# Transformer block in split float32: down operands formed as sums, six up tiles in seven products, one more product ahead of the last phase

## Chip, cores, metric

One core of a Trainium2 chip runs the program. The metric is device time in microseconds (us) of one execution, the median of several. The engines are TensorE (PE, with its weight loads PEld), VectorE (DVE), ScalarE (ACT), GpSimd (POOL) and SyncE (SP, which only issues DMAs here).

## What is computed

One layer of an encoder trunk, 512 tokens by 1024 columns, all in float32: three groups of attention heads, one output projection, a gated MLP with a depthwise convolution, and a gated embedding. The change lies in the MLP:

```python
def conv_gated_mlp(h, w_up, conv_w, conv_b, w_down):   # h 512x1024, w_up 1024x5632, w_down 2816x1024
    u = h @ w_up
    up = jnp.pad(u, ((0, 0), (CONV_WIDTH - 1, 0), (0, 0)))
    c = conv_b
    for j in range(CONV_WIDTH):                         # CONV_WIDTH = 3
        c = c + conv_w[j] * up[:, j:j + S]
    gate, val = jnp.split(c, 2, axis=-1)
    return (jax.nn.silu(gate) * val) @ w_down
...
    h = h + conv_gated_mlp(rms_norm(h, ln_ffn[i]), w_up[i], conv_w[i], conv_b[i], w_down[i])
    gate = jax.nn.sigmoid(rms_norm(h, ln_ple[i]) @ w_ple_gate[i])
    h = h + (p[i] @ w_ple_proj[i]) * gate
```

## The kernel before

**Split operands.** Every float32 operand of a product is split in two parts: `hi`, a rounded copy that ACT writes, and `lo`, the rest, which DVE writes (`split`, line 168). A product is three matmuls, hi·hi, hi·lo and lo·hi (`mm3`). So each weight tile goes through a chain: a load into a raw tile by SP, the copy on ACT, the subtraction on DVE, then PE. There are 6 raw tiles of 768 columns (`NRAW`, line 151) and 7 pairs of hi and lo. They are used in turn, so a load waits until the tile six places back has been split, and a split until the pair seven places back has been multiplied.

**Up projection.** It goes in 22 tiles `f` of 128 gate and 128 value columns. In a plain tile (`up_plain`, line 1237) each half is 8 blocks times 3 matmuls of 512 token columns: 48 matmuls from 2048 columns of weights, in three pieces. In a tile in seven products (`up_seven`, line 1261) the 2x2 block product of Strassen and Winograd stands in place of eight block products: 7 products of 12 matmuls with 256 columns, 84 in all. Its weights (`seven_weights`, line 1102) are 3584 columns in five raw tiles. Three adding transfers from HBM, issued by POOL, and four POOL additions of 256 columns form the sums among them. The products are accumulated in PSUM banks X, Y, Z and Z2; ACT copies them out and DVE adds them into SBUF tiles `su`. `SEVEN` (line 50) names the tiles done so: 5, 10 and 15. They are woven with plain tiles, a piece of a plain tile after the second (third product in program text), and so on.

**Convolution and left operands.** `ff_chain` starts each half on ACT and adds two taps on DVE (`c<-u`, or `c<-su` for a tile in seven products), then multiplies the halves. PSUM banks are few: two of kind z, two s, three t, one o. A plain tile's gate half stands in a z bank until its two taps have read it. Two tiles `f` and `f + 1` make one pair; `left` (line 1194) forms from it the seven left operands of the down projection, four of them sums `sm`, and splits them.

**Down projection.** The 22 tiles fall into four phases (`PHASES`, line 46: tiles 0 to 5, 6 to 11, 12 to 17, 18 to 21). For each phase and half `n` of the output columns there are seven products (`PRODUCTS`, line 937), each 18 matmuls of 256 columns (12 in phase 3), into banks X, Y, Z. Behind each product DVE adds the bank into the residual `h` (`add_h`); the next product in the same bank waits for that. Phase 0 and phase 1 are done in a block of 14 products each, in the middle of the up tiles; phases 2 and 3 together at the end, which I call the last phase. The right operands come from `down_weights` (line 1120): four blocks are loaded, and four differences t1 to t4 are made by POOL in place, each from tiles that earlier splits and differences have read. In phases 0 to 2 they lie in raw tiles of 768 columns; in phase 3 in tiles of 512 named `dn_a`, `dn_b`, `dn_t`.

**Order.** Every step is a `Task` with a cost, dependencies and slots. PE's order is the order in which the program makes the PE tasks. For the other engines a small planner (`trial`, line 1645, and the loop behind it) sets a fixed order from costs and due times. Each engine then runs its queue in order; POOL's queue holds sums and adding transfers alike, and a transfer's issue waits there for what it needs. The loop from line 1500 sets the order of up tiles: a tile of `SEVEN` starts when plain tiles are `AHEAD` (2) behind, and a down block when its tiles have been done for three tiles (`downs`). In front of phase 3 stand four products of phase 2: a1, t1, a2 of half 0 and a1 of half 1. Then `cols3` transposes `h` on PE (`n_t<-ident,h`) for the final gate, once the additions into its rows are made, and `gate` (`pg`, line 1565) follows.

Of the kernel before, what the change touches and what calls it, by code (L numbers as in the profile page):

```python
# [47 lines left out]
AHEAD = 2  # L48

SEVEN = (5, 10, 15)  # L50
# [3 lines left out]
def kernel(ctx: ExitStack, tc: tile.TileContext, x, xt0, xt, pt_in, small, g_ffn_in, bias_c,  # L54
# [875 lines left out]
    L1A, L2A, L2B, L3, L1, L2, L4 = range(7)  # L930
    G, LEFT = {}, {}

    def left_tiles(name):
# [3 lines left out]
    PRODUCTS = ((L1A, 0, "X", True), (L1, 4, "Y", True), (L2, 5, "X", False), (L4, 2, "Y", False),  # L937
                (L3, 6, "X", False), (L2A, 1, "Z", True), (L2B, 3, "X", False))
# [8 lines left out]

    ADDS = {0: ((0, 0),), 1: ((1, 1),), 2: ((0, 1),), 3: ((0, 1),), 4: ((1, 1),), 5: ((0, 0),), 6: ((1, 0),)}

    def add_h(n, j, acc):  # L950
        for b, c in ADDS[j]:
            dve.tensor_tensor(out=hblk(b, n, c), in0=hblk(b, n, c), in1=pv(acc), op=ALU.add)
# [90 lines left out]

    def split_of(w, deps=(), gain=None, group=None, i=0):

        w.hi_slot = Slot("hi") if group is None else group.slot
        makes = [w.hi_slot] if not w.hi_slot.users else []

        def do():
            w.hi, w.lo = split(w.t, w.n, gain, None if group is None else group.get(i, w.n))  # L1050

        w.split = Task("do", [AC(w.n), DV(w.n * (1 if gain is None else 1.12))], do, (w.load, *deps), makes, [w.raw] + ([] if makes else [w.hi_slot]))
        return w

    def again(r, name, deps):
# [8 lines left out]
        w.hi_slot = Slot("hi")  # L1064
        w.split = Task("do", [AC(w.n), DV(w.n)], do, (w.load, *deps), [w.hi_slot], [w.raw])
# [52 lines left out]
    RIGHT = {"a1": 0, "t1": 4, "t2": 5, "b2": 2, "t3": 6, "a2": 1, "t4": 3}  # L1118

    def down_weights(ph, n, name, tag="raw"):  # L1120

        m = w_down[ph].shape[4]
        src = {what: w_down[ph][n, i, j] for what, (i, j) in (("a1", (0, 0)), ("b1", (0, 1)), ("b2", (1, 1)), ("a2", (1, 0)))}
        raw = {what: tile_of(m, f"{name}_{what}", src.get(what), tag) for what in ("a1", "b1", "b2", "t2", "a2")}

        place = {what: what for what in raw}
        wrote, read = {what: [q.load] for what, q in raw.items()}, {what: [] for what in raw}

        def diff(what, to, a, b):

            a, b, place[what] = place[a], place[b], to

            def do():
                x, y, z = (raw[q].t[:, :m] for q in (to, a, b))
                pool.tensor_tensor(out=x, in0=y, in1=z, op=ALU.subtract)

            q = Task("do", [("pool", 0.3 + m * 0.0021)], do, wrote[a] + wrote[b] + wrote[to] + read[to], (),
                     list({raw[p].raw: 0 for p in (to, a, b)}))
            for p in (a, b):
                read[p].append(q)  # L1140
            wrote[to], read[to] = [q], []

        def take(what):
            if what in ("t1", "t2", "t3", "t4"):
                diff(what, *{"t1": ("a1", "b1", "a1"), "t2": ("t2", "b2", "t1"), "t3": ("b1", "b2", "b1"), "t4": ("a2", "a2", "t2")}[what])
            p = place[what]
            w = again(raw[p], f"{name}_{what}", wrote[p])
            read[p].append(w.split)
            return w

        return take
# [42 lines left out]
    def left(f):  # L1194
# [6 lines left out]
        def one():  # L1201
# [7 lines left out]
            tt(out=sm[:, 0], in0=r1[:, :H], in1=r1[:, H:], op=ALU.subtract)  # L1209
            tt(out=sm[:, 1], in0=r1[:, H:], in1=r2[:, H:], op=ALU.add)  # L1210
            act.copy(hi[:, L1A], r1[:, :H])
            act.copy(hi[:, L2A : L2B + 1], r2.rearrange("p (j c) -> p j c", j=2))

        def two():
            (r1, r2), (hi, lo), sm = v["r"], v["hl"], v["sm"]
            tt(out=sm[:, 2], in0=sm[:, 1], in1=r1[:, :H], op=ALU.subtract)
            tt(out=sm[:, 3], in0=r2[:, :H], in1=sm[:, 2], op=ALU.subtract)
            act.copy(hi[:, L3:], sm)

        def three():  # L1220
            (r1, r2), (hi, lo), sm = v["r"], v["hl"], v["sm"]
            tt(out=lo[:, L1A], in0=r1[:, :H], in1=f32(hi[:, L1A]), op=ALU.subtract)
            tt(out=lo[:, L2A : L2B + 1], in0=r2.rearrange("p (j c) -> p j c", j=2), in1=f32(hi[:, L2A : L2B + 1]), op=ALU.subtract)

        def four():
            (r1, r2), (hi, lo), sm = v["r"], v["hl"], v["sm"]
            tt(out=lo[:, L3:], in0=sm, in1=f32(hi[:, L3:]), op=ALU.subtract)
# [96 lines left out]
    class Down:  # L1324
# [6 lines left out]
        def product(self, what, phs=None, last=True):  # L1331

            j = tuple(RIGHT).index(what)
            li, ri, an, begins = PRODUCTS[j]
            assert ri == RIGHT[what]
# [23 lines left out]
            if last:  # L1359
                self.reads[an] = [Task("do", [DV(S)], lambda: add_h(self.n, j, self.accs[an]), [p], (), [self.slots[an]])]  # L1360
                H_ADDS[self.n, j] = self.reads[an][0]

    def down(ph, n, tags):
        d = Down((ph,), n, tags)
        for what in RIGHT:
# [104 lines left out]
    PLAIN = [f for f in range(2, NF) if f not in SEVEN]  # L1470
    plain = (f for f in PLAIN for _ in up_plain(f))
    at_f, pieces = [2], [0]
    DT = {"X": "t", "Y": "o", "Z": "t"}
    due = {}

    def count():

        for ph in due:
            due[ph] += 1
        for ph in range(2):  # L1480
            if ph not in due and all(f in done_f for f in range(PHASES[ph], PHASES[ph + 1])):
                due[ph] = 0

    def fill(n):
# [254 lines left out]
```

## Time and profile before

| | us |
|---|---|
| median of 3 runs (727.46 to 729.07) | 727.47 |
| the profiled execution | 727.97 |
| its span in the trace | 726.2 |
| PE, DVE, ACT, POOL busy | 706.1, 553.0, 393.8, 270.9 |
| up tiles begin | 314 |
| first down block | 430.7 to 460.7 |
| second down block | 515.4 to 545.8 |
| last phase | 620.0 to 676.0 |
| gate | 676.0 to the end |

How to read the rows that follow: `out<-in` names tiles with their numbers left out. All lines carry one line number, L78, that of the helper which issues every instruction, so they are told apart by their tiles: `u` and `pg` are plain up tiles and the gate, `sX`, `sY`, `sZ` the products of a tile in seven, `dn_X`, `dn_Y`, `dn_Z` the down products, `w_raw`, `w_hi`, `w_lo` weights on their way, `g_ah`, `g_al` (or `xh`, `xl` in the last phase) left operands. A matmul's duration in a row includes its way through the array. What a matmul takes of PE's time is read from start to start. DVE's instructions overlap by a little in the same way, so the sum of mean durations is a little above the busy time.

### The profile page before, as it was taken

Reading aid. Unit: us, or ns where it says so; the run is one execution under the profiler, and the core shown is the slowest. Engines: PE = TensorE matmul, PEld = TensorE weight load, DVE = VectorE, ACT = ScalarE, POOL = GpSimd, SP = SyncE. Lnnn points to the kernel's source line nnn. Section 1 sums busy time; section 2 is a strip of 40 time slices with the busy share of each in tenths; the row PEclk is TensorE's granted clock in tenths of the full one; section 3 lists DMA queues with packets and bytes.
Section 4 is the critical chain, followed back from the end, with each engine's and each line's share of the span. In section 5 each row is a group of like instructions: output and inputs, shape, how many; then the busy total and the mean of one; then the engine's idle time right before and its main releaser. Section 6 shows DMA issues by size and latency. Waiting matters only on the chain. (4 is left out here: it accounts for less than half of the span.)

```text
span 726.2 us, 11876 instructions
## 1 busy us (share of the span) xinstructions
PE 706.1 (97%) x4219; PEld 633.7 (87%) x4219; DVE 553.0 (76%) x1085; ACT 393.8 (54%) x745; POOL 270.9 (37%) x359
## 2 busy tenths in 40 slices
PE   9998999999999999999999999999999999999997
PEld 8987989998999887889888899888998888899886
DVE  7678787887877855758978768787898779988552
ACT  6646775865766664564655544543444543544821
POOL 5676676756665640212101144031520004361400
PEclk9999999999999999999999999999999999999999
DMA  9443425404211135564445434562254322123441
GB/s 332 172 136 110 120 63 124 138 30 110 88 48 56 59 63 165 171 210 90 138 138 125 102 100 123 139 159 66 88 175 117 95 87 82 57 73 94 156 129 58
DMA packets 36806, 83.22 MB, mean 115 GB/s; under 512 B 4198, under 2 KB 5990, under 8 KB 36748
## 3 DMA queue, kind: packets, MB, share of 16 engines
q1 hardware_dynamic: 32700, 73.52, 32.3%
q0 software_dynamic: 3760, 8.66, 6.4%
q8 instruction: 33, 0.54, 0.3%
q10 hardware_dynamic: 288, 0.30, 0.1%
q14 instruction: 25, 0.20, 0.1%
HBM read 74.19 MB, written 4.21 MB: 108 GB/s over the span
## 5 line engine op out<-in xcount | busy, mean ns | idle before, releaser
L78 DVE TENSOR_TENSOR w_lo<-w_raw,w_hi 128x768 fp32r<-128x768 f32 (+1 forms) x118 | 114.9, 993 | 21.9 <-ACT w_hi L78 21.2
L78 ACT CAST w_hi<-w_raw 128x768 fp32r<-128x768 f32 (+1 forms) x118 | 89.6, 786 | 71.1 <-POOL w_raw L78 33.0
L78 PE MATMUL u<-Tl,w_hi 128*128 128x512 f32 (+1 forms) x336 | 125.6, 374 | 0.8 <-DVE Tl L78 0.8
L78 PE MATMUL u<-Th,w_hi 128*128 128x512 f32 (+1 forms) x336 | 125.7, 374 | 0.6 <-ACT pps L78 0.6
L78 PE MATMUL u<-Th,w_lo 128*128 128x512 f32 (+1 forms) x336 | 125.4, 373 | 0.0
L78 POOL TENSOR_TENSOR w_raw<-w_raw,w_raw 128x768 f32<-128x768 f32 (+1 forms) x30 | 55.0, 1854 | 143.7 <-DVE w_lo L78 112.8
L78 PEld LDWEIGHTS u<-Tl,w_hi 128*128 128x128 f32 x336 | 63.1, 188 | 13.0 <-DVE Tl L78 1.2
L78 PEld LDWEIGHTS u<-Th,w_hi 128*128 128x128 f32 x336 | 63.1, 188 | 12.9 <-ACT pps L78 1.0
L78 PEld LDWEIGHTS u<-Th,w_lo 128*128 128x128 f32 x336 | 63.1, 188 | 12.5
L78 DVE SCALAR_TENSOR_TENSOR c<-u,cols,c 128x511 f32<-128x511 f32 x76 | 56.7, 747 | 18.6 <-ACT c L78 17.4
L78 POOL DMA_DIRECT2D w_raw<-in_w_up_dram x9 | 7.9, 912 | 100.2 <-DMA w_raw<-in_w_up_dram 100.2
L78 ACT ACTIVATE c<-u,cols 128x512 f32<-128x512 f32 x38 | 29.5, 776 | 21.7 <-PE u L78 21.7
L78 PE MATMUL dn_X<-w_hi,g_ah 128*128 128x256 f32 x144 | 40.7, 283 | 0.3 <-DVE h L78 0.3
L78 PE MATMUL dn_X<-w_lo,g_ah 128*128 128x256 f32 x144 | 40.7, 283 | 0.3 <-DVE w_lo L78 0.3
L78 PE MATMUL dn_X<-w_hi,g_al 128*128 128x256 f32 x144 | 40.6, 282 | 0.0
L78 PE MATMUL B_z<-B_h,Th 128*128 128x384 f32 x96 | 34.6, 360 | 0.6 <-DVE B_zn L78 0.6
L78 PE MATMUL C_z<-C_h,Th 128*128 128x384 f32 x96 | 34.3, 358 | 0.0
L78 PE MATMUL C_z<-C_l,Th 128*128 128x384 f32 x96 | 32.3, 337 | 0.0
L78 PE MATMUL B_z<-B_h,Tl 128*128 128x384 f32 x96 | 32.3, 337 | 0.0
L78 PE MATMUL C_z<-C_h,Tl 128*128 128x384 f32 x96 | 32.3, 337 | 0.0
L78 PE MATMUL B_z<-B_l,Th 128*128 128x384 f32 x96 | 32.3, 337 | 0.0
L78 PEld LDWEIGHTS dn_X<-w_hi,g_ah 128*128 128x128 f32 x144 | 27.1, 188 | 0.8 <-ACT w_hi L78 0.5
(484 smaller groups left out, 2145.6 us busy)
## 6 DMA issues: line engine op xcount, KB each, us to landing
w_raw<-in_w_up_dram SPq DMA_DIRECT2D x50, 384.0 KB, 3.7
w_raw<-in_w_down_dram SPq DMA_DIRECT2D x24, 384.0 KB, 3.1
w_raw<-in_w_up_dram SPq DMA_DIRECT2D x22, 256.0 KB, 3.4
B_r<-in_w_in_dram SPq DMA_DIRECT2D x12, 384.0 KB, 3.4
C_r<-in_w_in_dram SPq DMA_DIRECT2D x12, 384.0 KB, 3.2
wo_r<-in_w_out_dram SPq DMA_DIRECT2D x16, 256.0 KB, 2.9
w_raw<-in_w_ple_gate_dram SPq DMA_DIRECT2D x16, 256.0 KB, 2.9
h<-in_x_dram SPq DMA_DIRECT2D x4, 512.0 KB, 7.0
```

The lines of the kernel that those rows point to most:

```text
L78: ins = getattr(self.eng, op)(*a, **k)
```

## The change

- Tiles 4, 7, 9, 11, 13 and 15 are done in seven products instead of 5, 10 and 15.
- The order of pieces is one written string: P is a piece of a plain tile (three a tile), S one of a tile in seven (six), D one product of a down block. Between the two down blocks stand three plain tiles and three in seven, in alternation. The last 17 pieces are plain.
- The seven products of the down projection are formed another way. The right operands are named by sums of blocks: 1e, 1o, 2o as loaded, S1, 1e2e, S2 and 1oS2 as sums. In the 768-column phases S1 and 1e2e are made by an adding transfer from HBM onto a loaded block, S2 and 1oS2 by POOL; in phase 3 all four by POOL. Five blocks are loaded where four were. The signs go to the left operands and to `add_h`, which now also subtracts.
- In front of phase 3 stand five products of phase 2: 1e, S1, 1o of half 0, and 1e, S1 of half 1. The transposes `cols3` are placed elsewhere among the last products; those of the second half now stand between the last down product and the gate.

`LO_BY` is empty, so `lo_by_dma`, which is new too, is never used.

```diff
-AHEAD = 2
-
-SEVEN = (5, 10, 15)
+ORDER = ("PPPPSSPSSSPSPPPPSSPSSSPSPSSPSSSPSPDDDDDDDDDDDDDDSSPSSSPSPSSPSSSPSPSSPSSSPSPDDDDDDDDDDDDDDPPPPPPPPPPPPPPPPP")
...
+BY = {"S1": "dma", "1e2e": "dma", "S2": "pool", "1oS2": "pool"}
...
-    PRODUCTS = ((L1A, 0, "X", True), (L1, 4, "Y", True), (L2, 5, "X", False), (L4, 2, "Y", False),
-                (L3, 6, "X", False), (L2A, 1, "Z", True), (L2B, 3, "X", False))
+    PRODUCTS = {"1e": (0, "X", True, 1, 0, ALU.add), "S1": (3, "Y", True, 0, 1, ALU.subtract), "S2": (4, "X", False, 0, 0, ALU.add),
+                "1o": (2, "Z", True, 1, 0, ALU.add), "1e2e": (5, "X", False, 0, 1, ALU.subtract), "1oS2": (1, "Y", False, 0, 0, ALU.add),
+                "2o": (6, "X", False, 1, 1, ALU.subtract)}
...
     def down_weights(ph, n, name, tag="raw"):
...
-        def diff(what, to, a, b):
...
-                pool.tensor_tensor(out=x, in0=y, in1=z, op=ALU.subtract)
...
+        by = {what: BY[what] if tag == "raw" else "pool" for what in BY}
+        firsts = {"S1": "2e", "1e": "1e", "1o": "1o", "1e2e": "1e" if by["1e2e"] == "dma" else "2e", "2o": "2o"}
...
+        def add(what, to, other, before=()):
+            if by[what] == "dma":
+                v = (lambda: src[other]) if what in ("S1", "1e2e") else (lambda: raw[other].t[:, :m])
+                more = () if what in ("S1", "1e2e") else [raw[other].raw]
+                deps[what] = [add_of(raw[to], 0, m, v, before, more)]
+            else:
+                deps[what] = [sum_of(raw[to], 0, raw[other], 0, m, before)]
...
+            if what == "S2":
...
+                add("S2", "1e", "S1", [*deps["S1"], *deps.get("1e2e", ()), w["1e"].split])
+            if what == "1oS2":
+                add("1oS2", "1o", "1e", [*deps["S2"], w["1o"].split])
...
     def left(f):
...
-            tt(out=sm[:, 0], in0=r1[:, :H], in1=r1[:, H:], op=ALU.subtract)
-            tt(out=sm[:, 1], in0=r1[:, H:], in1=r2[:, H:], op=ALU.add)
+            tt(out=sm[:, 0], in0=r1[:, H:], in1=r1[:, :H], op=ALU.subtract)
+            tt(out=sm[:, 2], in0=r2[:, :H], in1=r1[:, :H], op=ALU.subtract)
...
-            tt(out=sm[:, 2], in0=sm[:, 1], in1=r1[:, :H], op=ALU.subtract)
-            tt(out=sm[:, 3], in0=r2[:, :H], in1=sm[:, 2], op=ALU.subtract)
+            dve.scalar_tensor_tensor(sm[:, 1], sm[:, 0], -1.0, r2[:, :H], ALU.mult, ALU.subtract)
+            dve.scalar_tensor_tensor(sm[:, 3], sm[:, 1], -1.0, r2[:, H:], ALU.mult, ALU.subtract)
...
+    FIRST = ("1e", "S1", "1o"), ("1e", "S1")
...
-    for what in ("a1", "t1", "a2"):
-        d0.product(what, (2,), False)
-    d1.product("a1", (2,), False)
-    for what in RIGHT:
-        d0.product(what, (3,) if what in ("a1", "t1", "a2") else None)
+    d0, d1 = DL
+    for what in PRODUCTS:
+        d0.product(what, (3,) if what in FIRST[0] else None)
+    d1.product("1e", (3,))
     cols3(0, 0)
     cols3(1, 0)
-    d1.product("a1", (3,))
+    d1.product("S1", (3,) if "S1" in FIRST[1] else None)
     cols3(2, 0)
-    d1.product("a2")
     cols3(3, 0)
-    for what in ("t1", "t2", "b2", "t3"):
+    for what in ("S2", "1o", "1e2e", "1oS2"):
         d1.product(what)
+    d1.product("2o")
     cols3(0, 1)
     cols3(1, 1)
-    d1.product("t4")
```

More of the change, by code (lines that the diff above doesn't have):

```diff
@@ L46, with tiles_of @@
 PHASES = (0, 6, 12, 18, 22)
-AHEAD = 2
-SEVEN = (5, 10, 15)
+ORDER = ("PPPPSSPSSSPSPPPPSSPSSSPSPSSPSSSPSPDDDDDDDDDDDDDDSSPSSSPSPSSPSSSPSPSSPSSSPSPDDDDDDDDDDDDDDPPPPPPPPPPPPPPPPP")
+def tiles_of(order):
+    f, n, tiles = 2, {"P": 0, "S": 0}, {"P": [], "S": []}
+    for c in order:
+        if c in n:
+            if n[c] == 0:
+                tiles[c].append(f)
+                f += 1
+            n[c] = (n[c] + 1) % {"P": 3, "S": 6}[c]
+    assert f == NF and not any(n.values()), (f, n)
+    return tiles["P"], tiles["S"]
+PLAIN, SEVEN = tiles_of(ORDER)
+LO_BY = ()
+BY = {"S1": "dma", "1e2e": "dma", "S2": "pool", "1oS2": "pool"}
 @with_exitstack
@@ L1331, in product @@
         def product(self, what, phs=None, last=True):
[L1333 to L1335 removed]
+            li, an, begins = PRODUCTS[what][:3]
             for ph in phs or self.phs:
```

136 lines of the change are left out of this document (64 added, 72 removed).

## Prediction

> **What bounds the kernel now.** I read the page's head first, then busy time by stage, then the waits, and last the instructions in order of time around each wait.
>
> ```profile
> span 726.2 us, 11876 instructions
> PE 706.1 (97%) x4219; PEld 633.7 (87%) x4219; DVE 553.0 (76%) x1085; ACT 393.8 (54%) x745; POOL 270.9 (37%) x359
> ```
>
> TensorE (PE) is busy for 97% of the span; the others have room on the average. The change touches only what follows the first up tiles: the changed program issues the same PE instructions in the same order until the middle of the up projection. These are that part's stretches (columns: length, busy time and instructions of PE, PEld, DVE, ACT, POOL, clock, DMA share, GB/s). The bounds are where the PE stream changes kind: up tiles 2 to 9, first down block, up tiles to the second block, that block, the remaining up tiles, the last phase.
>
> ```profile
> 339.60:430.70 91.10, 91.10 (x475) 77.19 (x474) 73.55 (x108) 47.75 (x73) 18.36 (x17) 1.00 0.46 123
> 430.70:460.70 30.00, 30.00 (x254) 29.95 (x253) 24.50 (x32) 12.41 (x17) 9.51 (x5) 1.00 0.51 156
> 460.70:515.40 54.70, 54.70 (x278) 45.91 (x278) 43.71 (x63) 27.75 (x42) 12.23 (x10) 1.00 0.37 96
> 515.40:545.80 30.40, 30.07 (x253) 29.90 (x252) 26.86 (x34) 12.57 (x17) 9.88 (x5) 1.00 0.52 155
> 545.80:620.00 74.20, 74.20 (x320) 59.68 (x319) 61.67 (x84) 33.45 (x50) 10.17 (x5) 1.00 0.33 96
> 620.00:681.00 61.00, 58.70 (x472) 56.78 (x470) 50.38 (x64) 31.48 (x50) 22.05 (x17) 1.00 0.26 83
> ```
>
> Up to 620 us PE has no gap worth the name, at full granted clock (1.00): there only fewer or shorter products help. The last phase is the one place where PE waits. VectorE (DVE) is next: 81% in the first stretch, 80% in the third.
>
> **The change, part by part.**
>
> *Three more up tiles in seven products.* A plain tile is 48 matmuls of 512 columns, a seven-product tile 84 of 256. The first row is 216 matmuls in one piece of the chain of work that ended last (start, us, what); the others are the first matmuls of neighbouring pieces around one seven-product tile (start, duration).
>
> ```profile
> 545.99 50.41 PE u L78 x216
> ```
>
> ```profile
> 409.58 0.28 PE L78 MATMUL sX<-Th,w_hi 128*128 128x256 f32 x1
> 413.83 0.39 PE L78 MATMUL u<-Th,w_hi 128*128 128x512 f32 x1
> 418.02 0.28 PE L78 MATMUL sY<-xh,w_hi 128*128 128x256 f32 x1
> 422.29 0.40 PE L78 MATMUL u<-Th,w_hi 128*128 128x512 f32 x1
> 425.09 0.28 PE L78 MATMUL sX<-xh,w_hi 128*128 128x256 f32 x1
> 426.51 0.44 PE L78 MATMUL u<-Th,w_hi 128*128 128x512 f32 x1
> ```
>
> 50.41 / 216 = 0.2334 us each, so 11.20 us for a plain tile. The seven-product tile takes (413.83 - 409.58) + (422.29 - 418.02) + (426.51 - 425.09) = 4.25 + 4.27 + 1.42 = 9.94 us. The difference is 1.26 us a tile, **3.8 us** for three. It lies wholly on the path, since PE has no gap there.
>
> Its price falls on the other engines. These are groups with shapes kept apart (count | busy us, mean ns | idle before).
>
> ```profile
> L78 DVE TENSOR_TENSOR w_lo<-w_raw,w_hi 128x768 fp32r<-128x768 f32 x92 | 97.5, 1074 | 18.7 <-ACT w_hi L78 18.2
> L78 DVE TENSOR_TENSOR w_lo<-w_raw,w_hi 128x512 fp32r<-128x512 f32 x26 | 18.4, 707 | 3.2 <-ACT w_hi L78 3.0
> L78 DVE SCALAR_TENSOR_TENSOR c<-u,cols,c 128x511 f32<-128x511 f32 x38 | 28.3, 746 | 17.4 <-ACT c L78 17.4
> L78 DVE SCALAR_TENSOR_TENSOR c<-su,cols,c 128x511 f32<-128x511 f32 x6 | 7.0, 1162 | 0.3 <-ACT c L78 0.3
> L78 DVE TENSOR_TENSOR su<-sX,su 128x256 f32<-128x256 f32 x12 | 4.8, 418 | 8.3 <-ACT su L78 8.3
> L78 DVE TENSOR_TENSOR c<-c,c 128x512 f32<-128x512 f32 x22 | 15.8, 716 | 0.3
> L78 DVE TENSOR_TENSOR g_al<-sm,g_ah 128x1024 fp32r<-128x1024 f32 x9 | 11.0, 1218 | 0.0
> L78 POOL TENSOR_TENSOR w_raw<-w_raw,w_raw 128x768 f32<-128x768 f32 x24 | 48.3, 2022 | 139.3 <-DVE w_lo L78 112.8 <-issue 21.7 <-DMA w_raw<-in_w_down_dram 4.4
> L78 POOL TENSOR_TENSOR w_raw<-w_raw 128x256 f32<-128x256 f32 x6 | 6.9, 1146 | 0.0
> L78 POOL DMA_DIRECT2D w_raw<-in_w_up_dram x9 | 7.9, 912 | 100.2 <-DMA w_raw<-in_w_up_dram 100.2
> ```
>
> A seven-product tile has two more splits of 768 columns (2 x 1.07), four sums out of PSUM (4 x 0.42), and taps from SBUF instead of PSUM (at most 0.42 longer, two such): about +4.7 us of DVE a tile. On POOL it has four sums of 256 columns (4 x 1.15) and three issues (3 x 0.91), 7.3 us. The tightest place is the third stretch, between the down blocks. It gets three plain and three seven-product tiles, where it had about four and one. So its PE time is 54.70 + 2 x 9.94 - 11.20 = 63.4 us. A plain tile costs DVE 2 x 1.07 + 0.71 + 4 x 0.75 + 0.72 = 6.5 us (splits, taps, the product), a seven-product one 11.2. Half a pair of left operands adds about 2, an estimate from its largest operation (1.22 of some 4). DVE gets 43.71 + 22.4 - 6.5 + 2 = 61.6 us: 97%. The second down block behind it can take up 30.40 - 26.86 = 3.5 us of lag. The first stretch only swaps one tile and goes to 78 of 90 us, 87%. These sums overstate a little, since neighbouring DVE instructions overlap, and splits without POOL at work are shorter:
>
> ```profile
> 353.69 4.16 DVE L78 TENSOR_TENSOR w_lo<-w_raw,w_hi 128x768 fp32r<-128x768 f32 x5
> 402.21 2.34 DVE L78 TENSOR_TENSOR w_lo<-w_raw,w_hi 128x768 fp32r<-128x768 f32 x2 [2.57 <-ACT w_hi L78]
> 401.64 1.05 POOL L78 TENSOR_TENSOR w_raw<-w_raw 128x256 f32<-128x256 f32 x1
> ```
>
> Five splits (one of them of 512) in 4.16 us are 0.83 each; two beside POOL's sums took 1.17 each. At 0.85 instead of 1.07 the third stretch falls to about 57 of 63.4 us, so I take no PE wait from DVE's sum there, and keep the upper end for a rival. *Beside these rows:* the Trainium skill, "SBUF — State Buffer", section "SBUF: two separate sides", says that VectorE operations with two SBUF inputs and GpSimd operations that read SBUF take a port pair as an exclusive lock, the loser blocking until the other is done. The rows agree in direction. By that rule POOL's twelve new sums in the up stretches would hold DVE for up to 12 x 1.15 = 13.8 us more, and the twelve sums that the down blocks lose would free 24 us.
>
> Each seven-product tile hands one PSUM bank over just in time: a plain tile that follows begins when the taps of the one before it have read their bank.
>
> ```profile
> 424.81 1.52 DVE L78 SCALAR_TENSOR_TENSOR c<-u,cols,c 128x511 f32<-128x511 f32 x2
> ```
>
> These taps end at 426.33, and PE starts at 426.51. There will be six such places instead of three. Nothing was lost at them so far, and a split queued ahead of the taps would cost 0.85 us: bounds 0 to 3 x 0.85; I take **0.5 us lost** in all, nearest to the row.
>
> *Down operands as sums.* Matmul count, DVE splits and additions into h stay: seven products a block half. Before, four POOL operations of 2.02 us made the operands, each waiting for an earlier split. Now two stay on POOL and two come as adding transfers, for the 768-column phases: per half 2 x 2.02 + 2 x 0.91 instead of 4 x 2.02 us of POOL. Per half there is one more load (five for four) and two adding transfers.
>
> ```profile
> w_raw<-in_w_down_dram SPq DMA_DIRECT2D x24, 384.0 KB, 3.1
> w_raw<-in_w_up_dram POOLq DMA_DIRECT2D x3, 384.0 KB, 5.2
> ```
>
> An operand made by transfer costs 3.1 + 5.2 us from the time its buffer is free, and the issue waits on POOL for the load, with the next half's sums queued behind it. The second half's S1 has the least room: its buffer is the first half's 1e, free only after that half's last sum (2.02). From there 2.0 + 3.1 + 5.2 and a split (1.07, and about as much on ACT) are 12.4 us. The product comes eight products of 18 x 0.118 = 2.13 us, so 17 us, after the block's start, while the sum before it can run about when the block starts. I take 0 and keep 0 to 2 us a block. DMA is busy for half the time in these blocks, so there is room for the added bytes. In the left operands two of four plain operations of 256 columns become three-input ones; at the taps' rate for half their columns (0.37) against 0.42 for a plain one that is no change.
>
> *One more product ahead of the last phase.* The waits and their places (start, duration; in brackets the idle time and what ended it):
>
> ```profile
> 630.14 0.38 PE L78 MATMUL dn_Y<-w_hi,xh 128*128 128x256 f32 x1
> 631.71 0.38 PE L78 MATMUL dn_Y<-w_lo,xh 128*128 128x256 f32 x1 [1.19 <-DVE w_lo L78]
> 633.11 0.28 PE L78 MATMUL dn_X<-w_hi,g_ah 128*128 128x256 f32 x1
> 633.68 0.39 PE L78 MATMUL dn_X<-w_lo,g_ah 128*128 128x256 f32 x1 [0.29 <-DVE w_lo L78]
> 651.52 0.28 PE L78 MATMUL dn_X<-w_hi,xl 128*128 128x256 f32 x1
> 652.61 0.65 PE L78 MATMUL n_t<-ident,h 128*128 128x128 f32 x4 [0.81 <-DVE h L78]
> ```
>
> From start to start, less the 0.12 that a matmul of 256 columns takes: 1.45 + 0.45 + 0.97 = 2.9 us. The first two are late splits, the first of an operand that POOL made at the last moment:
>
> ```profile
> 627.26 0.68 DVE w_lo L78
> 628.32 1.12 POOL dn_a L78
> 630.12 1.54 DVE w_lo L78
> ```
>
> The old difference had to wait for the split before it. The new sum S1 needs two loads only, and PE comes to it 2.13 us later, as five instead of four products stand ahead of phase 3. That is more than the 1.9 us of both waits. The third wait, transposes of h behind their last addition, goes because another product now stands between. What may be late next: X products now follow one Y or Z product of 12 matmuls (1.42 us), in which h's addition (0.68) must be made. Bounds: nothing saved to 2.9; I take **2.4 us**. The gate's first products now stand right behind the transposes, but they begin with columns that have been ready for long: nothing.
>
> *Sum.* The profiled execution took 727.97 us (span 726.2 and 1.77 around it), 0.5 above the median of 727.47. 3.8 + 2.4 - 0.5 = 5.7 less: **722.3 us**.
>
> **The rivals.**
>
> 1. *The tail's waits only move* (X, Z, X behind each other's additions, or POOL's phase 3 sums beside the splits). For it speaks DVE's 50.38 of 61 us there. Then only the products count: 727.97 - 3.8 + 0.5 = 724.7.
> 2. *The adding transfers are late* in both blocks, 2 us each: 722.3 + 4 = 726.3. For it: 5.2 against 3.1 us to landing, and POOL's in-order queue. Against: the product count above. The Trainium skill speaks for it in "DMA: Bandwidth & Descriptors", section "SWDGE vs HWDGE vs iDMA": accumulating transfers need descriptors that GpSimd writes, and VectorE can lock it out; the 0.91 us issues above do not show more than that.
> 3. *Slower: DVE becomes the bound in the third stretch.* In the trace DVE stood idle there for 54.70 - 43.71 = 11.0 us. If these waits, on ACT after PE, stay as long, and the work is 61.6, the stretch takes 72.6 instead of 63.4 us, 9.2 more; without the block's 3.5 us of spare (it has its own waits), the result is 722.3 + 9.2 = 731.5. It decides from about 7.5 us of lag on. Against it: most of these waits are DVE ahead of its work, and the shorter splits.
> 4. *All waits go and no hand-over costs*, the second block's 0.5 us too: 727.97 - 3.8 - 2.9 - 0.5 = 720.8; it is the low edge of the forecast.
>
> That the products do not shrink is no rival: the changed program issues 108 more matmuls, 3 x (84 - 48).
>
> **How the numbers follow.** The measurement of this kernel can tell about 0.3%, 2.2 us: faster is below 725.3, slower above 729.7. Forecast, with rival 4: 0.45 (720 to 723.7). Rival 1: 0.25 (724 to 725.5, about a tenth of that within 0.3%). Rival 2: 0.18 (half of it below 725.3, as one late block gives 724.3). Rival 3: 0.12, of which 0.10 slower. Faster: 0.45 + 0.22 + 0.08 = 0.75, same 0.15, slower 0.10. The range 719.5 to 728.0 leaves out rival 3 and a little on both ends.
>
> **What would show it.** Right: seven-product pieces at 0.118 us a matmul six times, PE gapless through both blocks, no dn_Y wait on w_lo, no n_t wait on h, PE's first gate product about 6 us earlier. Wrong: PE waiting for w_lo or for a bank (c) in the stretch between the blocks, DVE busy over 95% there; or a POOL or DMA releaser ahead of S1 or S2 splits in a block.

## The result, and the profile after

| | before | after |
|---|---|---|
| median, us | 727.46 (5 runs) | 731.77 (5 runs, 730.28 to 733.63) |
| ratio | 1 | 1.0060 (95%: 1.0046 to 1.0074) |
| profiled execution, us | 727.97 | 733.63 |

The change makes the kernel 0.6% slower; 722.3 was forecast, in a range up to 728.0. The head of the page after, then busy time by stage, cut as before (up tiles 2 to 9, first down block, up tiles to the second block, that block, the remaining up tiles, the last phase):

```profile
span 731.8 us, 12191 instructions
PE 704.4 (96%) x4327; PEld 637.3 (87%) x4327; DVE 560.4 (77%) x1103; ACT 400.5 (55%) x763; POOL 277.2 (38%) x383
```

```profile
339.30:429.40 90.10, 90.10 (x513) 78.13 (x512) 79.65 (x114) 49.49 (x78) 24.87 (x24) 1.00 0.59 150
429.40:462.40 33.00, 30.27 (x253) 29.98 (x252) 25.19 (x31) 10.75 (x14) 8.89 (x9) 1.00 0.69 181
462.40:531.80 69.40, 66.04 (x399) 58.02 (x398) 58.84 (x83) 38.60 (x63) 20.14 (x21) 0.98 0.58 154
531.80:564.70 32.90, 30.16 (x254) 29.98 (x253) 24.31 (x32) 13.12 (x18) 6.04 (x5) 1.00 0.62 187
564.70:627.65 62.95, 62.95 (x271) 50.56 (x271) 52.44 (x75) 29.71 (x44) 11.88 (x8) 1.00 0.41 112
627.65:686.40 58.75, 57.66 (x471) 56.59 (x469) 47.40 (x65) 30.59 (x50) 14.64 (x14) 1.00 0.37 120
```

The six lengths add up to 347.10 us, against 341.40 before: 5.7 more, which is the whole difference of the profiled executions (5.66). The medians are only 4.3 apart: the profiled execution of the changed kernel is the slowest of its five. Stage by stage: first stretch 1.0 less, no gap; the two blocks 3.0 and 2.5 more; the two other up stretches together 132.35 instead of 128.90, where two seven-product tiles more should have made 126.4, so 6.0 lost; the last phase 2.25 less. PE is idle for 2.7 us in each block and 3.4 us between them (length less PE busy), where before it had 0.3 us in all. DVE is at 85% between the blocks: it is not the bound.

Each block has one wait. PE and VectorE, ScalarE and GpSimd around the first, and PE at the second (start, duration, in brackets the idle time before and what ended it):

```profile
442.08 0.28 PE L97 MATMUL dn_Y<-w_hi,g_al 128*128 128x256 f32 x1
445.09 0.36 PE L97 MATMUL dn_X<-w_hi,g_ah 128*128 128x256 f32 x1 [2.73 <-DVE h L97]
...
547.49 0.36 PE L97 MATMUL dn_X<-w_hi,g_ah 128*128 128x256 f32 x1 [2.74 <-DVE h L97]
```

```profile
441.92 1.83 DVE L97 TENSOR_TENSOR w_lo<-w_raw,w_hi 128x768 fp32r<-128x768 f32 x1 [3.98 <-ACT w_hi L97]
443.67 0.68 DVE L97 TENSOR_TENSOR h<-h,dn_Z 128x512 f32<-128x512 f32 x1
444.27 0.67 DVE L97 TENSOR_TENSOR h<-h,dn_X 128x512 f32<-128x512 f32 x1
```

```profile
432.77 0.88 POOL L97 DMA_DIRECT2D w_raw<-in_w_down_dram  x1 [3.30 <-DMA w_raw<-in_w_down_dram]
435.00 0.86 POOL L97 DMA_DIRECT2D w_raw<-in_w_down_dram  x1 [1.36 <-DMA w_raw<-in_w_down_dram]
```

```profile
441.05 0.84 ACT L97 CAST w_hi<-w_raw 128x768 fp32r<-128x768 f32 x1 [8.48 <-DMA w_raw<-in_w_down_dram]
```

```profile
w_raw<-in_w_down_dram SPq DMA_DIRECT2D x30, 384.0 KB, 3.5
w_raw<-in_w_down_dram POOLq DMA_DIRECT2D x12, 384.0 KB, 5.9
```

Read backwards: PE, about to write product 2o into bank X, waits for the addition of 1e2e into h, which reads that bank. That addition has its operands, but in VectorE's queue it stands behind the split of the second half's S1. VectorE is idle for 3.98 us there, waiting for ScalarE's rounding of S1, and ScalarE for S1's adding transfer, issued at 432.77 and landed 8.2 us later, at 441.0. (The one issued at 435.00 is 1e2e's; it landed at 442.6.) In the second block S1's transfer took 8.2 us too, from 535.20 to 543.4. The median of all twelve, 5.9 us in the last row, hides this. The planner, which writes the queues, reckons 0.9 + 768 x 0.0025 + 2.0 = 4.8 us, so it saw the split ready first. PE itself comes to S1's product only two products later.

The longest wait between the blocks, on VectorE, GpSimd and PE:

```profile
499.32 3.76 DVE L97 TENSOR_TENSOR w_lo<-w_raw,w_hi 128x768 fp32r<-128x768 f32 x1 [0.31 <-ACT w_hi L97]
503.01 1.52 DVE L97 SCALAR_TENSOR_TENSOR c<-u,cols,c 128x511 f32<-128x511 f32 x2
```

```profile
499.12 1.07 POOL L97 TENSOR_TENSOR w_raw<-w_raw 128x256 f32<-128x256 f32 x1
499.82 1.75 POOL L97 TENSOR_TENSOR w_raw<-w_raw,w_raw 128x256 f32<-128x256 f32 x2
501.20 1.06 POOL L97 TENSOR_TENSOR w_raw<-w_raw 128x256 f32<-128x256 f32 x1
```

```profile
502.08 0.28 PE L97 MATMUL sX<-xh,w_lo 128*128 128x256 f32 x1
504.67 0.47 PE L97 MATMUL u<-Th,w_hi 128*128 128x512 f32 x1 [2.31 <-DVE c L97]
...
505.45 0.58 PE L97 MATMUL u<-Th,w_hi 128*128 128x512 f32 x1
505.83 0.63 PE L97 MATMUL u<-Tl,w_hi 128*128 128x512 f32 x1
506.26 0.63 PE L97 MATMUL u<-Th,w_lo 128*128 128x512 f32 x1
...
508.82 0.43 PE L97 MATMUL u<-Th,w_lo 128*128 128x512 f32 x1
```

One split took 3.76 us where the same shape mostly takes 0.95; it ends 0.8 us after GpSimd's four sums. Behind it in the queue stand the taps that free PE's bank: PE waits 2.6 us from start to start. After the wait comes a second loss: between 505.45 and 508.82 eight matmuls of 512 columns start 0.42 apart instead of 0.233, 1.5 us more.

In the last phase the old waits on w_lo and n_t's on h are gone; a new one of 1.1 us stands at 647.4, product 1e2e behind h, whose addition waits for a split of 2.04 us beside GpSimd's sums.

### The profile page after: what moved, and what is told of

Same layout as the page of the kernel before. It is cut to its first block, busy times and chain, and to the rows that moved or that the text cites. A ratio compares the mean times of both kernels' runs of the same rounds, so it can differ in the third digit from the quotient of the medians.

```text
span 731.8 us, 12191 instructions
## 1 busy us (share of the span) xinstructions
PE 704.4 (96%) x4327; PEld 637.3 (87%) x4327; DVE 560.4 (77%) x1103; ACT 400.5 (55%) x763; POOL 277.2 (38%) x383
## 4 chain that ended last, share of the span: by engine, by line
PE 64%; DVE 14%; DMA 9%; issue 4%; POOL 4%; ACT 4%; SPq 0%; DVEq 0%; POOLq 0%; ACTq 0%
PE u L97 19%; PE C_z L97 6%; PE pg L97 6%; PE wo L97 4%; PE dn_X L97 4%; PE B_z L97 4%; DVE w_lo L97 3%; DMA w_raw<-in_w_down_dram 3%; DMA w_raw<-in_w_up_dram 3%; PE sX L97 3%; PE sY L97 2%; PE sZ L97 2%; PE dn_Y L97 2%; DVE c L97 1%; PE pp L97 1%
## 5 line engine op out<-in xcount | busy, mean ns | idle before, releaser
L97 PE MATMUL u<-Th,w_hi 128*128 128x512 f32 (+1 forms) x288 | 107.6, 374 | 3.0 <-DVE c L97 2.3
L97 PE MATMUL u<-Tl,w_hi 128*128 128x512 f32 (+1 forms) x288 | 107.3, 372 | 0.8 <-DVE Tl L97 0.8
L97 PE MATMUL u<-Th,w_lo 128*128 128x512 f32 (+1 forms) x288 | 106.9, 371 | 0.5 <-DVE w_lo L97 0.5
L97 PEld LDWEIGHTS u<-Th,w_hi 128*128 128x128 f32 x288 | 54.3, 189 | 13.8 <-issue 2.7
L97 PEld LDWEIGHTS u<-Th,w_lo 128*128 128x128 f32 x288 | 54.4, 189 | 11.2 <-DVE w_lo L97 0.9
L97 PEld LDWEIGHTS u<-Tl,w_hi 128*128 128x128 f32 x288 | 54.4, 189 | 10.6 <-DVE Tl L97 1.2
L97 POOL TENSOR_TENSOR w_raw<-w_raw,w_raw 128x256 f32<-128x256 f32 (+1 forms) x24 | 37.7, 1605 | 55.5 <-DVE w_lo L97 32.5
L97 DVE SCALAR_TENSOR_TENSOR c<-u,cols,c 128x511 f32<-128x511 f32 x64 | 47.7, 745 | 13.5 <-ACT c L97 12.6
L97 POOL DMA_DIRECT2D w_raw<-in_w_up_dram x18 | 15.8, 908 | 96.3 <-DMA w_raw<-in_w_up_dram 87.1
L97 POOL DMA_DIRECT2D w_raw<-in_w_down_dram x12 | 10.5, 872 | 79.2 <-DMA w_raw<-in_w_down_dram 79.2
```

What stands on the lines that cost most here:

```text
L97: ins = getattr(self.eng, op)(*a, **k)
```

## Experiments

**Theory.** A: the waits in the blocks are the queue order behind a late adding transfer. B: between the blocks GpSimd's sums hold VectorE's splits up. C: after some waits PE runs at half speed for a while. **Rivals:** VectorE is the bound; seven-product tiles or the bytes cost by themselves. The ratios, with 95% intervals, are to the kernel before on the same chip. Differences to the changed kernel are of medians that were not taken side by side; the kernel before came to 727.46 to 728.03 us beside them. noadd, nosums and neither leave out part of the computation.

| run | median, us (runs) | ratio to before |
|---|---|---|
| noadd | 724.91 (6) | 0.9955 (0.9938 to 0.9973) |
| nosums | 728.12 (11) | 1.0000 (0.9992 to 1.0009) |
| neither | 721.63 (4) | 0.9913 (0.9898 to 0.9928) |
| three | 734.07 (5) | 1.0085 (1.0071 to 1.0099) |
| six_old | 730.68 (12) | 1.0036 (1.0023 to 1.0048) |
| fill | 731.81 (5) | 1.0051 (1.0037 to 1.0065) |
| later_cost | 729.23 (11) | 1.0015 (1.0004 to 1.0026) |
| three_cost | 729.50 (9) | 1.0026 (1.0016 to 1.0036) |
| three_c65 | 725.86 (12) | 0.9973 (0.9964 to 0.9982) |
| no_extra | 736.58 (5) | 1.0127 (1.0109 to 1.0146) |
| extra_only | 725.87 (10) | 0.9971 (0.9961 to 0.9981) |
| mended | 735.38 (4) | 1.0103 (1.0089 to 1.0116) |
| all_cost | 734.23 (6) | 1.0091 (1.0072 to 1.0109) |
| spread_cost | 733.47 (6) | 1.0076 (1.0057 to 1.0094) |
| apart | 729.67 (7) | 1.0028 (1.0016 to 1.0039) |
| apart_a | 730.61 (5) | 1.0042 (1.0029 to 1.0055) |
| four_old | 725.85 (9) | 0.9973 (0.9963 to 0.9983) |
| four_c65 | 726.07 (7) | 0.9975 (0.9965 to 0.9986) |

### The two causes, taken away

**noadd**

```diff
 add_of, called with down=True for the down operands:
-            pool.dma_start(out=w.t[:, c0:c1], in_=src(), accum_op=ALU.add)
+            if not down:
+                pool.dma_start(out=w.t[:, c0:c1], in_=src(), accum_op=ALU.add)
```

> The changed kernel with the adding transfers of the down operands not issued, everything else in the same order; S1 and 1e2e are then their first summand alone, so part of the computation is left out. Theory A (in each down block the adding transfer of the second half's S1 lands late, its split stands ahead of h's addition in VectorE's queue, and PE waits for that addition, about 3 us a block): about 5.5 us below the changed kernel, 726.3 us, and no PE wait on h of over 0.5 us in the blocks. Rival (VectorE is simply the bound with six seven-product tiles): the splits stay, so 731 to 732 us. Rival (the loss is in the bytes on the DMA queues): between, as only 8 of 42 down transfers go.

724.91 us, 6.9 below the changed kernel; no PE wait on h of 0.5 us or more in the blocks, which last 29.9 us each. Theory A holds; VectorE as the bound does not, since its splits all stayed. In the profiled execution (723.74, 9.9 below that of the changed kernel) the bank wait between the blocks was absent too: here the same four sums (496.7 to 499.9 us) ran beside the taps, which took 1.53 us as ever, and not beside the split. The six executions spread from 722.03 to 726.43; whether the bank wait stands in the longer ones, no trace shows. The edit takes out all twelve adding transfers, the last phase's four with them.

**nosums**

```diff
 sum_of, of 256 columns (H) in a seven-product tile alone:
+            if n == H:
+                return
             d = w.t[:, c0 : c0 + n]
             pool.tensor_tensor(out=d, in0=d, in1=w2.t[:, c1 : c1 + n], op=ALU.add)
```

> The changed kernel with GpSimd's four sums in each seven-product tile not issued, everything else in the same order; two of the operands are then wrong sums, so part of the computation is left out. Theory B (GpSimd's back-to-back sums hold VectorE's splits up, which delays the taps and the hand-over of a PSUM bank, after which the granted clock drops): 3 to 6 us below the changed kernel, 726 to 729 us, with no PE wait on c of over 0.5 us between the blocks and no split of 768 columns longer than 2 us there; the waits in the two down blocks stay at 2.7 us each. Rival (VectorE is bound by its own work, whatever GpSimd does): within 1 us of 731.8 us.

728.12 us, 3.7 below the changed kernel. The split and the taps of the same place, VectorE of nosums:

```profile
497.96 0.96 DVE L97 TENSOR_TENSOR w_lo<-w_raw,w_hi 128x768 fp32r<-128x768 f32 x1 [0.31 <-ACT w_hi L97]
499.03 1.53 DVE L97 SCALAR_TENSOR_TENSOR c<-u,cols,c 128x511 f32<-128x511 f32 x2
```

0.96 instead of 3.76 us, and PE has no wait on c: theory B. A miss: the block waits did not stay at 2.7 us, they were 1.7 and 1.6; the adding transfers of the down operands landed after 5.0 us in the median, not 5.9, and the second half's S1 after 6.8 and 6.7, not 8.2. So the 3.7 us are not B alone.

**neither** (both edits)

> The changed kernel with neither the adding transfers of the down operands nor GpSimd's four sums in the seven-product tiles issued, everything else in the same order (noadd and nosums together; part of the computation is left out). If the two losses are separate: 731.8 - 6.9 - 3.7, about 721 us, near the forecast of 722.3. If they share a cause (GpSimd's queue, through which the transfers are issued and in which the sums stand): 723 to 725 us. If a third loss is left: over 725 us.

721.63 us, 10.1 below the changed kernel, against 6.9 + 3.7. Both blocks last 29.9 us and the stretch between them 63.5, where 63.4 was foreseen. The two are the whole difference to the forecast (722.3).

### One part of the change at a time

**three**

```diff
-ORDER = ("PPPPSSPSSSPSPPPPSSPSSSPSPSSPSSSPSPDD...DDSSPSSSPSPSSPSSSPSPSSPSSSPSPDD...DDPP...")
+ORDER = ("PPPPSSPSSSPSPPPPPPPPPPSSPSSSPSPDD...DDPPPPPPPPPSSPSSSPSPDD...DDPP...")
```

> The changed kernel with only three seven-product tiles, in the place and weave of the kernel before; the down operands and the extra product in front of the last phase as changed. If the losses in the blocks come from the adding transfers (theory A): tiles 0, blocks about +5.5, last phase about -1.8, so 731 us, and little loss between the blocks. Rival (the losses in the blocks come from the larger number of seven-product tiles around them): 725 to 726 us.

734.07 us. The waits in the blocks are there without the extra tiles, as theory A says (2.98 and 2.63 us), and nothing is lost between the blocks. The time is 3 us above 731, because here both waits are followed by matmuls at half speed.

**six_old**

```diff
-SEVEN = (5, 10, 15)
+ORDER = (as in the changed kernel)
```

> The kernel before with the six seven-product tiles in the changed kernel's weave, but with its old down operands (four differences on GpSimd a half) and its old last phase. Theory B: tiles -3.8, between the blocks +4 to +6, last phase 0, so 728 to 730 us, with a PE wait on a bank between the blocks. Rival (all losses hang on the adding transfers of the down operands): 723 to 724.5 us.

730.68 us, though these tiles shorten PE's work by 3.8. VectorE of six_old shows the same split, with the old down operands:

```profile
496.17 3.55 DVE L92 TENSOR_TENSOR w_lo<-w_raw,w_hi 128x768 fp32r<-128x768 f32 x1 [0.31 <-ACT w_hi L92]
499.64 1.52 DVE L92 SCALAR_TENSOR_TENSOR c<-u,cols,c 128x511 f32<-128x511 f32 x2
```

So loss B belongs to the additional tiles. More than half of what is lost in the profiled execution is not B: the stretch between the blocks is 66.5 us, 3.1 over the 63.4 foreseen, but the last phase is 60.3 instead of 56.0, with several small waits and then a granted clock of 0.50 at 634 to 638 us. Why these waits come with six tiles stays open.

**no_extra**

```diff
-    FIRST = ("1e", "S1", "1o"), ("1e", "S1")
+    FIRST = ("1e", "S1", "1o"), ("1e",)
```

> The changed kernel without the one more product in front of the last phase (S1 of the second column half goes back behind the transposes). If this product is what took the old waits away: the tail loses 1.5 to 3 us again, 733.3 to 735 us. Rival (the sums as operands took them away, since S1 needs two loads only): 731 to 732 us.

736.58 us, 4.8 above the changed kernel and over the 3.2 at most that was expected. In its profile waits on w_hi and w_lo are back in the last phase, which is 4.0 us longer up to the gate; the rest is half speed behind both block waits, for 6.8 and 3.4 us, which the changed kernel's profiled execution did not have.

**extra_only**

```diff
 the kernel before:
     d1.product("a1", (2,), False)
+    d1.product("t1", (2,), False)
...
     cols3(1, 0)
     d1.product("a1", (3,))
+    d1.product("t1", (3,))
...
-    for what in ("t1", "t2", "b2", "t3"):
+    for what in ("t2", "b2", "t3"):
```

> The kernel before with the third part of the change alone: the second operand's product of the second column half (its first difference) also runs once in front of the last phase, and its phase 3 part stands between the transposes. If the product in front is what takes the waits in the last phase away: of 2.9 us, 1.5 to 2.9 go, so 725 to 726.5 us. Rival (here the operand is a difference that GpSimd makes behind a split, so that the wait only moves to it): 727.5 to 728.5 us.

725.87 us: 2.1 less than before from the product alone. That settles the third part: the product in front gains this without the sums.

### Queue order in the blocks

**later_cost**

```diff
-        return Task("add", [("pool", 0.9), ("acc", (c1 - c0) * 0.0025)]
+        return Task("add", [("pool", 0.9), ("acc", (c1 - c0) * (0.0050 if down else 0.0025))]
```

> The changed kernel with one number changed: the planner reckons an adding transfer of a down operand at 2.0 us longer (6.7 instead of 4.8 us for 768 columns), so that VectorE's queue has h's additions after 1o and 1e2e ahead of the split of the next half's S1. The transfers themselves stay as late as they are. Theory A (order of VectorE's queue behind a late transfer): the two waits of 2.7 us in the blocks go, about 726 us; the split is done at some 444 us, and PE needs it from about 446.5 us on. Rival (the transfer itself is too late for PE): the waits move to S1's split, 729 us or more. Between the blocks nothing changes: the wait for c stays.

729.23 us. VectorE of later_cost in the first block:

```profile
438.48 0.69 DVE L97 TENSOR_TENSOR h<-h,dn_Z 128x512 f32<-128x512 f32 x1 [0.19 <-PE dn_Z L97]
...
440.62 0.69 DVE L97 TENSOR_TENSOR h<-h,dn_X 128x512 f32<-128x512 f32 x1 [0.79 <-PE dn_X L97]
441.80 1.83 DVE L97 TENSOR_TENSOR w_lo<-w_raw,w_hi 128x768 fp32r<-128x768 f32 x1 [0.49 <-ACT w_hi L97]
```

The additions now stand ahead of the split, the transfers of S1 are as late as they were (7.7 and 8.2 us), and the waits in the blocks fall from 2.7 us to 0.4 and 0.9. But "between the blocks nothing changes" was wrong. The whole plan shifted: the bank wait went, and a wait of 3 us came behind the block, with half speed for 6.8 us behind it. PE and ScalarE there:

```profile
467.62 0.80 PE L97 MATMUL u<-Th,w_hi 128*128 128x512 f32 x1 [2.98 <-ACT w_hi L97]
```

```profile
463.80 1.05 ACT L97 CAST g_ah<-sm 128x1024 fp32r<-128x1024 f32 x1 [3.96 <-DVE sm L97]
464.75 2.81 ACT L97 CAST w_hi<-w_raw 128x768 fp32r<-128x768 f32 x4
```

The roundings that PE needs stand in ScalarE's queue behind one that waits for VectorE.

**three_cost** and **three_c65**: three with this edit, and with 0.0065 in place of 0.0050.

> The kernel called three (three seven-product tiles, down operands and last phase as changed) with the planner's longer adding transfer of later_cost in the down blocks. Theory A with the clock: of the 734.1 us go the two block waits (3.1 and 2.8 us) and the slow matmuls behind them (1.6 and 1.5 us), 9 us in all, so 725 to 726.5 us, faster than the kernel before. Rival (the wait only moves to the next instruction of a queue, as it did behind the first block in later_cost): 728 us or more.

729.50 us, a miss: waits of 2.2 and 1.0 us on h were left. In this weave 0.0050 moved only the addition of 1o ahead of the split in the first block, not that of 1e2e.

> As three_cost with a still longer adding transfer (0.0065 instead of 0.0050 us a column), by which h's addition of 1e2e stands ahead of the late split in both blocks; at 0.0050 it still stood behind it (waits of 2.4 and 1.1 us). Theory A: those 3.5 us go, 729.5 - 3 = 726 to 727 us, a little faster than the kernel before. Rival (the adding transfers cost PE time whatever the queue order, the wait moves to the split): 728.5 us or more.

725.86 us, with one wait of 0.5 us left in the blocks. S1's transfers are as late as ever (7.6 and 7.8 us); one number of the planner differs from three, and with it the order of the queues, and that is worth 8.2 us with the clock behind it. The new operands then cost nothing and, beside extra_only's 725.87, gain nothing.

### The clock

**fill** (on three)

```diff
+                if ph < 2 and (what, self.n) == ("2o", 0):
+                    plain_do = do
+
+                    def do(ph=ph):
+                        FILL[ph] = bank("t", f"fill_{ph}")
+                        for _ in range(20):
+                            pe.transpose(FILL[ph][:, 0:P], ident, ident)
+                        plain_do()
```

> The kernel called three with 20 transposes of the identity into a free bank put in front of product 2o of the first half in each down block, where PE waits about 3 us for h. If the matmuls behind that wait run at half speed because PE stood idle (17 and 16 slow matmuls, 1.6 us a block in the profile of three): the filled gap keeps the clock, 3.2 us less than 734.1, 730.9 us. If the slow matmuls have another cause: 734 us, or a little more where the transposes do not fit the wait.

731.81 us, 2.3 below three (3.2 expected). The matmuls behind both waits, first three, then fill (columns as above; the clock stands ahead of the last two):

```profile
446.60:450.60 4.00, 3.95 (x21) 3.98 (x22) 3.36 (x5) 1.40 (x3) 1.63 (x1) 0.59 0.00 0
535.80:539.20 3.40, 3.40 (x17) 3.40 (x18) 3.03 (x4) 1.32 (x3) 1.11 (x1) 0.53 0.01 2
```

```profile
447.50:451.50 4.00, 3.95 (x33) 3.98 (x34) 4.00 (x6) 1.41 (x3) 1.63 (x1) 1.00 0.01 4
535.40:538.80 3.40, 3.33 (x28) 3.37 (x29) 3.40 (x5) 1.41 (x3) 1.01 (x1) 1.00 0.01 2
```

With idle PE the granted clock is 0.53 to 0.59 for some 3.4 us and 21 matmuls run in 4 us; with transposes in the gap it is 1.00 and 33 run. The half speed comes from the idle time: theory C.

### Six tiles, mended

**mended** (later_cost, and the four sums on VectorE)

```diff
-            pool.tensor_tensor(out=d, in0=d, in1=w2.t[:, c1 : c1 + n], op=ALU.add)
+            (dve if n == H else pool).tensor_tensor(out=d, in0=d, in1=w2.t[:, c1 : c1 + n], op=ALU.add)
```

> The changed kernel with two mends: the planner's longer adding transfer of the run later_cost, and the four sums of a seven-product tile on VectorE (4 x about 0.45 us a tile) instead of GpSimd. Theories A and B together: blocks -5.8, between the blocks -3 to -4, so 722 to 723.5 us. Rival (VectorE has no room for 1.8 us more a tile between the blocks): waits for splits or c there, 726 us or more.

735.38 us, a clear miss. PE waits 7.54 us at 473.1 for a rounding, and runs at half speed for 10.2 us behind it. This is not because VectorE is full: it stands idle for 4.7 us in front of the first sum, which waits for an up tile's adding transfer. Landing times of mended between 446 and 476 us:

```profile
w_raw<-in_w_up_dram SPq DMA_DIRECT2D x9, 384.0 KB, 3.5
...
w_raw<-in_w_up_dram POOLq DMA_DIRECT2D x1, 384.0 KB, 8.5
w_raw<-in_w_up_dram POOLq DMA_DIRECT2D x1, 256.0 KB, 8.8
w_raw<-in_w_up_dram POOLq DMA_DIRECT2D x1, 128.0 KB, 8.8
```

Three adding transfers issued together before the end of the block, at 454.9 to 456.4 us, all land after 8.5 to 8.8 us; twelve loads were issued in these 30 us, nine of them of 384 KB.

**all_cost** (0.0050 for every adding transfer) and **spread_cost** (the same, and in ORDER `DD...DD PPP` + two seven-product tiles + `DD...DD` + one seven-product tile):

> The changed kernel with the planner's longer adding transfer everywhere, in the up tiles too (0.9 + 0.0050 n + 2.0 us instead of 0.9 + 0.0025 n + 2.0). If the wait of 3 us behind the first block in later_cost comes from up transfers that land later than the planner reckons: it goes, with its slow matmuls, and the time is 723 to 726 us. Rival (the transfers are late for PE whatever the order, since three issued together land after 8.5 us): 727.5 us or more, the wait behind the block stays.

734.23 us: the wait behind the first block is 4.0 us, and again three adding transfers were issued together.

> As all_cost, with another weave: one whole plain tile right behind the first down block, and the last of the three seven-product tiles of the stretch between the blocks moved behind the second block. If the late up transfers are what PE waits for behind the block, a plain tile there (no adding transfers, 11.2 us) gives them time, and GpSimd and VectorE have less to do between the blocks: 721.5 to 724.5 us. Rival (VectorE's or ScalarE's queue order makes new waits wherever the tiles stand): 727 us or more.

733.47 us: no wait behind the first block, where the plain tile stands, and 3.95 us behind the second, where now a seven-product tile stands. With this setting the wait goes with a seven-product tile right behind a block; the place alone does not make it, since the changed kernel has one there and waits 0.5 us at most.

**apart** (later_cost; `DD...DD PPP` + one seven-product tile + `PPP` + one + `DD...DD PPP` + one) and **apart_a** (without the middle `PPP`):

> Six seven-product tiles with the new operands, the planner's cost of later_cost for the down blocks, and a weave in which a whole plain tile stands behind each down block and between the two seven-product tiles of the middle stretch (the sixth tile stands behind the second block). In all_cost and spread_cost the 4 us wait stood just where a seven-product tile begins behind a block, its three adding transfers having been issued together at the block's end. If that place is the cause: no wait over 1.5 us, and with the six tiles 722 to 724.5 us. Rival (the sums and late transfers cost as much wherever the tiles stand): 727 us or more.

> As apart, without the plain tile between the two seven-product tiles of the middle stretch. If neighbouring seven-product tiles there cost a wait by themselves (GpSimd's sums of the one beside VectorE's work of the other): 1 to 3 us more than apart; if only the place behind a block matters: as apart, 722 to 724.5 us.

729.67 and 730.61 us, not 722 to 724.5. The up stretches are clean now: no wait of 0.5 us in apart, 0.6 and 0.3 us on c in apart_a. But a new wait of 3.5 us stands in front of phase 3, as the last seven-product tile moved the left operands closer to the end (argued, not tested), with half speed for 3.4 and 6.8 us behind it. PE and ScalarE of apart:

```profile
630.74 0.38 PE L97 MATMUL dn_Y<-w_hi,g_ah 128*128 128x256 f32 x1 [3.50 <-ACT w_hi L97]
```

```profile
628.91 1.04 ACT L97 CAST xh<-sm 128x1024 fp32r<-128x1024 f32 x1 [2.87 <-DVE sm L97]
629.86 0.83 ACT L97 CAST w_hi<-w_raw 128x768 fp32r<-128x768 f32 x1
```

The pattern is that of later_cost: a rounding whose data are there stands behind one that waits for VectorE. With six tiles each mend moved the wait.

**four_old** and **four_c65**: extra_only and three_c65 with one more seven-product tile in the first stretch.

> extra_only (old down operands, one more product in front of the last phase) with one more seven-product tile, in the first stretch, where the changed kernel ran three of them without a gap: 725.9 - 1.26 = 724.6 us. Rival (any further seven-product tile costs a wait on a bank or an operand): 725.5 us or more.

> three_c65 (new down operands, h's additions ahead of the late split) with one more seven-product tile in the first stretch: 725.9 - 1.26 = 724.6 us. Rival (the order of VectorE's queue falls otherwise with another weave and the block waits are back): 727.5 us or more.

725.85 and 726.07 us: no gain, though the first stretch is shorter. four_old's profile has a wait on w_lo of 0.9 us in the last phase where extra_only's has 0.2; four_c65's has 0.3 us on c where three_c65's has none, and 0.3 us less on h, so where its 1.26 us went stays open. No run that computes everything beat extra_only and three_c65 beyond the intervals; these beat both kernels.

## Why the prediction was wrong

- *Six seven-product tiles, 3.8 us less work:* right. The first stretch has no gap and is 1.0 us shorter for one tile more, and neither, without the two losses, came to 721.63.
- *"I take 0 and keep 0 to 2 us a block"* for the adding transfers: the first step that failed. The transfer's 5.2 us was too small for the operand that counts: S1 of the second half landed after 8.2 us in both blocks, and its split ended 14.3 us after the first block's start. The count of products still held, since by it PE comes to S1's own product only at 17 us. What was left out is who stands behind its split in VectorE's in-order queue: h's addition, for which PE waits. 3.0 and 2.5 us (theory A, noadd, later_cost, three_c65). Rival 2 had the late transfer but took the wait for S1's own. Why these transfers take 8.2 us and those of the first half 4.5 to 6.1 stays open. The sentence from the Trainium skill, "DMA: Bandwidth & Descriptors", section "SWDGE vs HWDGE vs iDMA", that VectorE can lock GpSimd out of writing descriptors, does not explain it by what the trace shows: the issues in the blocks took 0.86 to 0.88 us, against 0.91 before, and VectorE stood idle for the last 3 us of S1's transfer in the first block.
- *"so I take no PE wait from DVE's sum there"*: the sum was right (85% busy) and the conclusion wrong. A wait needs no full engine: one split held for 3.76 us, with a bank's release behind it, made it. Rival 3 forecast 731.5, near the result, but by luck: it went by VectorE's sum, which nosums and neither refute, since the splits stayed and the time went.
- *"I take 0.5 us lost"* for the hand-overs, bounded by 0.85 each: 2.6 us at one of them. The bound used a free split. The Trainium skill, "SBUF — State Buffer", section "SBUF: two separate sides", was in the prediction with up to 13.8 us of holding against 24 us freed, and moved no term of the sum. The split of 3.76 us over four sums, and 0.96 us without them, agree with its exclusive lock.
- *The last phase, 2.4 us:* right in size (2.25 by stages; 2.1 in extra_only), with one new wait where rival 1 had it.
- *The clock at 1.00* was taken as given. 1.5 us of the difference, and in three and no_extra more, is half speed after a wait.

Added up: 5.7 less was forecast and 5.7 more came, 11.4 apart. Of these 5.5 are the blocks, 5.5 the other up stretches (6.0 lost, 0.5 foreseen; 3.4 of it idle, 1.5 half speed, the rest matmuls around the waits that start later), 0.3 the first stretch and 0.15 the last phase.

## What to carry to other kernels

For every transfer that becomes later, list what stands behind its consumer on that engine's in-order queue, and who waits for that; the consumer itself may have slack and its neighbour none. Where a planner writes the queues, give it landing times with a margin before judging a new kind of transfer: it reckoned 4.8 us where 8.2 were measured, and the order was mended only when it reckoned 7.9. Read the landing of the one transfer on the path, not the median of its kind, which was 5.9 us here. Take a gap in a matmul stream at more than its length.

## What was not expected of the hardware

- A gap of 2.4 to 3.6 us, from start to start, in an otherwise full matmul stream can halve the granted clock for about 3.4 us (no_extra, the changed kernel, three) or twice as long (later_cost, no_extra); in the changed kernel this cost 1.5 us more than the gap itself. It does not always: behind both 3.0 us gaps in the blocks of the changed kernel the clock stayed at 1.00, behind three's 3.3 and 2.9 us it fell both times. The Trainium skill, "TensorE: Matmul & The Clock Gate", Part 1, has a free-running window of about 3.4 us after which the clock falls or rises; the stretches of half speed, 3.4, 6.8 and 10.2 us long, agree. It asks for an idle window of that length before the clock falls, and here shorter gaps were enough: the measurement decides. That the window runs by itself may be why equal gaps differ, which no run here shows.
- In the changed kernel an adding transfer of 384 KB for the up or down weights lands 4.5 to 8.2 us after its issue (medians 5.2 and 5.9), a plain load of the same size after 4.0 and 3.5 in the median; three together took 8.5 to 8.8 us in mended.
- GpSimd's sums, back to back, held one VectorE split for all four of them, not for one: it started 0.2 us after the first sum, took 3.76 us and ended 0.8 us after the last; in six_old the same split took 3.55.
